# Low parts of 24 weight chunks: a difference on VectorE replaced by a negative on ScalarE and an adding transfer

## The chip, the cores and the metric

The kernel runs on one core of a Trainium2 chip. The metric is the device time of one execution in microseconds (us). The kernel before has a median of 847.87 us over three runs (847.83, 847.87 and 848.68).

## What is computed

One decoder layer for 512 positions of width 1024, in float32: a normalised input goes through one combined projection, three branches use it, their gated sum is projected back and added, and a gated feed-forward part with 2816 hidden columns follows. Cut to what matters here:

```python
h = rmsnorm(x, norm_mix)
qkv_a, a_a, b_a, z_a, glu_in, q_c, gate_logits = split(h @ w_in)
# branch A: gated delta rule on convolved q, k, v, in chunks of 64 (a triangular solve in each)
y_a = (rmsnorm(o_a, gdn_norm) * silu(z_a)) @ w_gdn_out
# branch B: gated linear unit, depthwise convolution of 31 taps, layernorm
y_b = silu(layernorm(conv31(u))) @ w_cc_out
# branch C: attention of 4 heads into mem (256 positions)
y_c = softmax(q_c k_m / sqrt(128)) v_m @ w_xa_out
x = x + (sum of sigmoid(gates) * y) @ w_o
x = x + (silu(conv3(W_g h)) * (W_v h)) @ w_down
return rmsnorm(x, norm_final)
```

## The kernel before

Activations lie in SBUF transposed, 128 features by 512 positions to a tile, and weights come from HBM as 128x128 tiles. A float32 product is made of three matmuls on rounded operands of type float32r: high weight with high activation, high with low, low with high (`proj`, L271 to L273). The high part is the value rounded to float32r, and the low part is what the rounding leaves of it.

So each weight tile is needed as a high and a low part. The array `wall` holds all weights but those of the last projection in the order of their use, as 124 chunks of eight tiles, 128x1024 numbers or 512 KB. `fetch` (L232 to L253) loads a chunk with SP's queue into a `raw` tile (L243), and the helper `split` (L146 to L154) makes the two parts: ACT casts `raw` into `whi` (L150), DVE subtracts `whi` from `raw` into `wlo` (L151). There are four `raw` tiles and four pairs of `whi` and `wlo`, used in turn. `wtile` (L255) calls `fetch` four chunks ahead of the chunk in use, so a pair is written again from the time on at which the chunk four places earlier has been multiplied. Eight tiles of a chunk are 24 matmuls.

The order of PE and of SP's queue is that of the program's text. It is written by generators that are stepped together (`run`), where the projections are the main line and the smaller matmuls of the branches are put between their tiles. The orders of DVE, ACT and POOL come out of the compiler's scheduler, which goes by the dependences and by its own costs.

Chunks with the numbers 22 to 45, counted from 0, hold the second half of the weights of `k`, then those of `q`, `v` and `z` of branch A, and most of the chunks that mix the gates of branch C with its output weights. Their loading and splitting falls in the time from about 97 to 259 us. What else runs there, by line:

- Softmax of the attention scores: DVE's maximum (L523, L524), ACT's exponentials `e` (issued by the helper at L140), DVE's scaling (L530). The transposed probabilities are split into `pTh` on ACT and `pTl` on DVE and multiplied with the values at L549 to L551.
- The gates `gl` of the convolution branch on ACT, `u` on DVE (L598), and 31 taps for each of four tiles on DVE (`cc`, L608). Exponentials and the sigmoid of `gl` need different tables on ACT, so table loads stand between them.
- The decay matrices `dec` of branch A: DVE at L501, exponentials on ACT, a factor on POOL (L712).
- Norms of `k`: POOL's `pow` (L683), DVE's products, and `rows` (L305), which casts a small tile `c` (L308), subtracts (L309) and transposes both on PE (L313).
- The base inverse (L749 to L766): a chain of multiplications and subtractions on the tile `ti` on DVE, which solves the 32x32 triangles. SP stores the result to HBM (L768, L769) and loads it in another layout (L772). `invert` copies it on ACT and POOL (`tm`, `tt`, L794 to L799), makes small products on PE, copies them (`m`, L807) and multiplies again on PE (L813, L814).

Of the kernel before, what the change touches and what calls it, by code (L numbers as in the profile page):

```python
# [11 lines left out]
AF = mybir.ActivationFunctionType  # L12
ALU = mybir.AluOpType
AX = mybir.AxisListType

P = 128
# [4 lines left out]
WAIT = {"mem": 4, "x": 30, "decay": 15, "scores": 1, "level": 6, "scan": 3, "out": 8,  # L21
        "k": 20, "head": 7, "krow": 6, "inverse": 16, "store": 5, "load": 14, "z": 4, "kk": 1, "ln": 30, "mix": 0}
WARM = 10

EARLY = 8

# [33 lines left out]
def hybrid_kernel(ctx: ExitStack, tc: tile.TileContext, xT, memT, xtok, mtok, wall, wdn, nfin, vecs, cms, y):  # L60
# [15 lines left out]
    def nm(p):  # L76
        uid[0] += 1
        return f"{p}{uid[0]}"
# [21 lines left out]
    def G(shape=(P, S)):  # L100
        return psg.tile(list(shape), F32, name=nm("g"), tag="g")
# [4 lines left out]
    A, G_, PE = nc.scalar, nc.gpsimd, nc.tensor  # L106
# [40 lines left out]
    def split(src, hi, lo, scale=None, eng=V):  # L147

        if scale is None:
            A.copy(hi, src)  # L150
            eng.tensor_tensor(lo, src, f(hi), op=ALU.subtract)  # L151
        else:
            A.activation(hi, src, AF.Copy, scale=scale)
            V.scalar_tensor_tensor(lo, src, scale, f(hi), op0=ALU.mult, op1=ALU.subtract)  # L154
# [39 lines left out]
    def vc(n, i=0, w=1):  # L194
        o = VOFF[n][0]
        return vec[:, o + i:o + i + w]
# [16 lines left out]
    ps = G()  # L213
    for _ in range(WARM):
        PE.matmul(ps[:, :P], warm[:, P:2 * P], warm[:, :P], start=True, stop=True)
# [16 lines left out]
    def fetch(upto):  # L232
        if upto > NW and beyond[0]:
            beyond[0](2 * (upto - NW))
        while state[0] < min(upto, NW):
            c = state[0]
            raw = wraw.tile([P, 8 * P], F32, name=nm("raw"), tag="raw")
            n = 4 * P if c < QC else 8 * P
            for o in range(0, 8 * P, n):
                if c < QC:  # L240
                    k = 2 * c + o // n
                    nc.sync.dma_start(x[k], xT[:, k])
                nc.sync.dma_start(raw[:, o:o + n], wall[c][:, o:o + n])  # L243
            hi = wsp.tile([P, 8 * P], F32R, name=nm("whi"), tag="whi")
            lo = wsp.tile([P, 8 * P], F32R, name=nm("wlo"), tag="wlo")
            for o in range(0, 8 * P, n):
                c_ = slice(o, o + n)
                if c < QC:
                    k = 2 * c + o // n
                    split(x[k], xh[k], xl[k], vc("nmix", k))  # L250
                split(raw[:, c_], hi[:, c_], lo[:, c_], eng=nc.vector)
            chunks[c] = (hi, lo)
            state[0] += 1  # L253

    def wtile(i, n=1):  # L255

        fetch(i // 8 + AHEAD)
        hi, lo = chunks[i // 8]
        o = (i % 8) * P
        return hi[:, o:o + n * P], lo[:, o:o + n * P]  # L260
# [74 lines left out]


    fetch(QC)
    nc.sync.dma_start(cm[:, :P], cms[:, :P])
    rx, rm = C((P, NT)), C((P, 2))
# [17 lines left out]
    for i in range(4):  # L357
        nc.sync.dma_start(mraw[i], memT[:, 2 * i:2 * i + 2])
        for k in range(2):
            split(mraw[i][:, k], mh[i][:, k], ml[i][:, k], vc("nmem", 2 * i + k))  # L360
        if i == 1:
            fetch(QC + 1)
# [1029 lines left out]
```

## Time and profile before

| | |
|---|---|
| median of three runs | 847.87 us |
| the profiled execution's own time | 850.48 us |
| its span, first to last instruction | 848.7 us |
| mean granted clock of TensorE | 0.995 |
| DMA traffic | 123.22 MB |

The profile is that of one execution. Busy time of an engine is the time in which it had an instruction under way. In the profile's lists, a group or an instruction names line, engine, operation and its tiles as output<-inputs. A bracket such as [0.41 <-DVE pTl L151] gives the engine's idle time before the instruction and what ended it. The granted clock (PEclk) is 1.00 at full speed.

### The profile page before, as it was taken

Reading aid. Unit: us, or ns where it says so; the run is one execution under the profiler, and the core shown is the slowest. Engines: PE = TensorE matmul, PEld = TensorE weight load, DVE = VectorE, ACT = ScalarE, POOL = GpSimd, SP = SyncE. Lnnn points to the kernel's source line nnn. Section 1 sums busy time; section 2 is a strip of 40 time slices with the busy share of each in tenths; the row PEclk is TensorE's granted clock in tenths of the full one; section 3 lists DMA queues with packets and bytes.
Section 4 is the critical chain, followed back from the end, with each engine's and each line's share of the span. In section 5 each row is a group of like instructions: output and inputs, shape, how many; then the busy total and the mean of one; then the engine's idle time right before and its main releaser. Section 6 shows DMA issues by size and latency. Waiting matters only on the chain.

```text
span 848.7 us, 11144 instructions
## 1 busy us (share of the span) xinstructions
PE 837.2 (99%) x4140; PEld 695.1 (82%) x4140; DVE 606.3 (71%) x954; ACT 388.0 (46%) x669; POOL 87.6 (10%) x101
## 2 busy tenths in 40 slices
PE   9999999999999999999999999999999999999996
PEld 7888788788887888888888888888888888888885
DVE  5885799859988999683266556666666656769863
ACT  7854675534235345452334344333333333657443
POOL 0100002500020001032000031111120110000001
PEclk9999999999999999999999999999999999999998
DMA  9753212242063122322244469696896882275662
GB/s 320 294 183 125 75 51 75 78 121 100 25 166 108 51 75 75 100 74 100 100 149 149 149 163 234 182 209 169 211 222 161 229 206 99 76 222 174 223 186 99
DMA packets 60949, 123.22 MB, mean 145 GB/s; under 512 B 18048, under 2 KB 20352, under 8 KB 60544
## 3 DMA queue, kind: packets, MB, share of 16 engines
q1 hardware_dynamic: 47424, 107.84, 38.0%
q0 software_dynamic: 6336, 11.54, 9.0%
q10 hardware_dynamic: 7136, 3.15, 1.3%
q8 instruction: 32, 0.52, 0.3%
q14 instruction: 21, 0.17, 0.1%
HBM read 118.83 MB, written 26.74 MB: 172 GB/s over the span
## 4 chain that ended last, share of the span: by engine, by line
PE 94%; DVE 4%; issue 1%; ACT 1%; POOL 0%; POOLq 0%; DVEq 0%; ACTq 0%
PE mm L271 19%; PE mm L272 18%; PE mm L273 18%; PE g L272 5%; PE g L273 5%; PE g L271 5%; PE g L1261 2%; PE g L1262 2%; PE g L1263 2%; PE mm L1262 2%; PE mm L1261 2%; PE mm L1263 2%; DVE wlo L151 1%; PE g L570 1%; PE g L572 1%
## 5 line engine op out<-in xcount | busy, mean ns | idle before, releaser
L150 ACT CAST whi<-raw 128x1024 fp32r<-128x1024 f32 (+1 forms) x167 | 171.6, 1028 | 277.1 <-PE mm L272 167.9
L151 DVE TENSOR_TENSOR wlo<-raw,whi 128x1024 fp32r<-128x1024 f32 (+1 forms) x167 | 201.3, 1205 | 77.5 <-ACT whi L150 76.6
L271 PE MATMUL mm<-hh,whi 128*128 128x512 f32 x352 | 142.6, 405 | 0.0
L273 PE MATMUL mm<-hh,wlo 128*128 128x512 f32 x352 | 137.6, 391 | 0.0
L272 PE MATMUL mm<-hl,whi 128*128 128x512 f32 x352 | 137.4, 390 | 0.0
L608 DVE SCALAR_TENSOR_TENSOR cc<-u,vec,cc 128x507 f32<-128x507 f32 (+19 forms) x120 | 86.7, 732 | 1.0
L273 PEld LDWEIGHTS mm<-hh,wlo 128*128 128x128 f32 x352 | 66.1, 188 | 14.3
L271 PEld LDWEIGHTS mm<-hh,whi 128*128 128x128 f32 x352 | 66.3, 188 | 13.1 <-issue 1.5
L272 PEld LDWEIGHTS mm<-hl,whi 128*128 128x128 f32 x352 | 66.4, 189 | 11.5
L271 PE MATMUL g<-fh,whi 128*128 128x512 f32 x176 | 69.1, 392 | 0.0
L271 PE MATMUL mm<-fh,whi 128*128 128x512 f32 x176 | 68.9, 392 | 0.0
L273 PE MATMUL mm<-fh,wlo 128*128 128x512 f32 x176 | 68.6, 390 | 0.0
L273 PE MATMUL g<-fh,wlo 128*128 128x512 f32 x176 | 68.6, 390 | 0.0
L272 PE MATMUL g<-fl,whi 128*128 128x512 f32 x176 | 68.6, 390 | 0.0
L272 PE MATMUL mm<-fl,whi 128*128 128x512 f32 x176 | 68.6, 390 | 0.0
L1096 POOL DMA_DIRECT2D q<-wdn x44 | 36.3, 1000 | 160.1 <-DMA q<-q 97.2
L1163 DVE TENSOR_TENSOR fg<-mm,rfb 128x512 f32<-128x512 f32 x22 | 15.2, 691 | 52.1 <-PE mm L273 52.1
L273 PEld LDWEIGHTS mm<-fh,wlo 128*128 128x128 f32 x176 | 33.1, 188 | 6.9
L273 PEld LDWEIGHTS g<-fh,wlo 128*128 128x128 f32 x176 | 33.0, 188 | 6.9
L272 PEld LDWEIGHTS mm<-fl,whi 128*128 128x128 f32 x176 | 33.1, 188 | 6.7
L271 PEld LDWEIGHTS mm<-fh,whi 128*128 128x128 f32 x176 | 33.0, 188 | 6.8
L271 PEld LDWEIGHTS g<-fh,whi 128*128 128x128 f32 x176 | 33.1, 188 | 6.7
(311 smaller groups left out, 1586.4 us busy)
## 6 DMA issues: line engine op xcount, KB each, us to landing
raw<-wall SPq DMA_DIRECT2D x120, 512.0 KB, 3.4
q<-wdn POOLq DMA_DIRECT2D x44, 256.0 KB, 6.4
raw<-q SPq DMA_DIRECT2D x44, 256.0 KB, 2.9
raw<-wdn SPq DMA_DIRECT2D x33, 256.0 KB, 3.4
q<-wdn SPq DMA_DIRECT2D x22, 256.0 KB, 4.5
q<-q SPq DMA_DIRECT2D x22, 256.0 KB, 4.9
x<-xT SPq DMA_DIRECT2D x16, 256.0 KB, 3.9
raw<-wall SPq DMA_DIRECT2D x8, 256.0 KB, 5.5
```

The source lines that it names most:

```text
L150: A.copy(hi, src)
L151: eng.tensor_tensor(lo, src, f(hi), op=ALU.subtract)
L271: PE.matmul(ps, hi, xh[k], start=(k == 0), stop=False)
L272: PE.matmul(ps, hi, xl[k], start=False, stop=False)
L273: last[0] = PE.matmul(ps, lo, xh[k], start=False, stop=(k == n - 1))
L570: PE.matmul(ps[h], hi, xh[k], start=(k == 0), stop=False)
L608: paced(V.scalar_tensor_tensor(a[:, s:], u[c][:, :S - s], vc("dww", c * 31 + 30 - s), a[:, s:], op0=ALU.mult, op1=ALU.add))
L1096: paced(G_.dma_start(dst[p - 3], b[p - 3], accum_op=ALU.add))
L1163: V.tensor_tensor(g, ps, rfb, op=ALU.mult)
L1261: PE.matmul(ps[m], h[:, o:o + P], hi, start=(p == 0), stop=False)
L1262: PE.matmul(ps[m], h[:, o:o + P], lo, start=False, stop=False)
L1263: last[0] = PE.matmul(ps[m], l[:, o:o + P], hi, start=False, stop=(p == NP - 1))
```

## The change

For the chunks 22 to 45, ACT casts the high part as before, then writes the negative of the raw chunk into the low tile, rounded to float32r. A transfer issued by POOL then reads the chunk a second time from HBM and adds it onto that negative. The sum is the rounding's remainder. DVE's subtraction of these chunks falls away, and `raw` comes free when ACT has read it twice. The other chunks stay as they were. In the changed kernel, the lines after L24 have numbers 2 higher, and those from L246 on 6 higher.

```diff
+ADDED = range(22, 46)
...
             hi = wsp.tile([P, 8 * P], F32R, name=nm("whi"), tag="whi")
             lo = wsp.tile([P, 8 * P], F32R, name=nm("wlo"), tag="wlo")
-            for o in range(0, 8 * P, n):
+            if c in ADDED:
+                A.copy(hi, raw)
+                A.activation(lo, raw, AF.Copy, scale=-1.0)
+                G_.dma_start(lo, wall[c], accum_op=ALU.add)
+            for o in range(0, 0 if c in ADDED else 8 * P, n):
                 c_ = slice(o, o + n)
```

The orders of PE and SP's queue stay. The scheduler lays out ACT, DVE and POOL anew. Three places of this follow. Names carry running numbers, which are one or a few higher in the changed kernel (`whi_1239` is `whi_1240` there).

The first is on ACT, from the exponentials of the decay matrices to the next gate. `e` are exponentials of the scores, with table loads around `gl`. Before:

```order
L140 ACTIVATE dec_884<-dec_884 128x512
L140 ACTIVATE dec_885<-dec_885 128x512
L140 ACTIVATE dec_886<-dec_886 128x512
L140 ACTIVATE e_1129,c_1130<-g_1119,c_1126 128x256 x2
L150 CAST whi_1239<-raw_1237 128x1024
L140 ACTIVATE e_1164,c_1165<-g_1154,c_1161 128x256 x2
L140 ACTIVATE e_1191,c_1192<-g_1181,c_1188 128x256 x2
L150 CAST pTh_1249<-g_1253 128x512
L140 ACTIVATE e_1214,c_1215<-g_1204,c_1211 128x256 x2
L140 ACT_TABLE_LOAD
L140 ACTIVATE gl_1221<-mm_1094,vec 128x512
L150 CAST pTh_1251<-g_1268 128x512
```

In the changed kernel, from the table load ahead of the decay matrices:

```order
L142 ACT_TABLE_LOAD
L142 ACTIVATE e_1130,c_1131<-g_1120,c_1127 128x256 x2
L142 ACTIVATE dec_883<-dec_883 128x512
L142 ACTIVATE dec_884<-dec_884 128x512
L142 ACTIVATE dec_885<-dec_885 128x512
L142 ACTIVATE dec_886<-dec_886 128x512
L249 CAST whi_1240<-raw_1238 128x1024
L250 ACTIVATE wlo_1241<-raw_1238 128x1024
L142 ACTIVATE e_1165,c_1166<-g_1155,c_1162 128x256 x2
L142 ACTIVATE e_1192,c_1193<-g_1182,c_1189 128x256 x2
L142 ACTIVATE e_1215,c_1216<-g_1205,c_1212 128x256 x2
L142 ACT_TABLE_LOAD
```

The pair that stood behind `dec` (`e_1129`, now `e_1130`) is now ahead of it, the scaled copy `wlo_1241` stands behind the cast of its chunk, the last pair of exponentials has moved ahead of the table load, and `pTh_1249` (now `pTh_1251`) follows behind the next `gl` with the other `pTh`.

The second is on DVE, at the end of the base inverse. `ti` and `tmp` are the inverse, `cc` taps of the convolution. Before:

```order
L118 TENSOR_TENSOR tmp_2102<-blk_1855,ti_1849 128x32
L151 TENSOR_TENSOR wlo_2332<-raw_2329,whi_2331 128x1024
L608 SCALAR_TENSOR_TENSOR cc_2277<-u_532,vec,cc_2277 128x504
L118 TENSOR_TENSOR ti_1849<-ti_1849,tmp_2102 128x32
L608 SCALAR_TENSOR_TENSOR cc_2277<-u_532,vec,cc_2277 128x503
L118 TENSOR_TENSOR tmp_2102<-blk_1855,ti_1849 128x16
L608 SCALAR_TENSOR_TENSOR cc_2277<-u_532,vec,cc_2277 128x502
L118 TENSOR_TENSOR ti_1849<-ti_1849,tmp_2102 128x16
L608 SCALAR_TENSOR_TENSOR cc_2277<-u_532,vec,cc_2277 128x501
L118 COPY tit_2165<-ti_1849 128x512
L608 SCALAR_TENSOR_TENSOR cc_2277<-u_532,vec,cc_2277 128x500
L608 SCALAR_TENSOR_TENSOR cc_2277<-u_532,vec,cc_2277 128x499
```

In the changed kernel:

```order
L120 TENSOR_TENSOR tmp_2118<-blk_1866,ti_1860 128x64
L120 TENSOR_TENSOR ti_1860<-ti_1860,tmp_2118 128x64
L120 TENSOR_TENSOR tmp_2118<-blk_1866,ti_1860 128x48
L120 TENSOR_TENSOR ti_1860<-ti_1860,tmp_2118 128x48
L120 TENSOR_TENSOR tmp_2118<-blk_1866,ti_1860 128x32
L120 TENSOR_TENSOR ti_1860<-ti_1860,tmp_2118 128x32
L614 SCALAR_TENSOR_TENSOR cc_1262<-u_487,vec,cc_1262 128x486
L120 TENSOR_TENSOR tmp_2118<-blk_1866,ti_1860 128x16
L614 SCALAR_TENSOR_TENSOR cc_1262<-u_487,vec,cc_1262 128x485
L120 TENSOR_TENSOR ti_1860<-ti_1860,tmp_2118 128x16
L120 COPY tit_2181<-ti_1860 128x512
L614 SCALAR_TENSOR_TENSOR cc_1262<-u_487,vec,cc_1262 128x484
```

The subtraction into `wlo` is gone, and the operations of the inverse stand next to each other where taps stood between them.

The third is POOL's queue, from its last operation ahead of the chunks. `c` with `mhalf` is the `pow` of the norms of `k`. Before:

```order
L298 TENSOR_TENSOR c_193<-c_287,mhalf 128x2
L683 TENSOR_TENSOR c_1225<-c_1225,mhalf 128x4
L742 MEMSET ti_1849 128x512
L747 MEMSET ti_1849 64x16 x2
L683 TENSOR_TENSOR c_1225<-c_1225,mhalf 128x4 x3
L712 TENSOR_TENSOR dec_883<-dec_883,c_1225 128x512
```

In the changed kernel:

```order
L304 TENSOR_TENSOR c_193<-c_287,mhalf 128x2
L251 DMA wlo_1098<-wall 128x1024
L251 DMA wlo_1241<-wall 128x1024
L251 DMA wlo_1313<-wall 128x1024
L251 DMA wlo_1384<-wall 128x1024
L689 TENSOR_TENSOR c_1226<-c_1226,mhalf 128x4
L748 MEMSET ti_1860 128x512
L753 MEMSET ti_1860 64x16 x2
L251 DMA wlo_1469<-wall 128x1024
L689 TENSOR_TENSOR c_1226<-c_1226,mhalf 128x4
L251 DMA wlo_1554<-wall 128x1024
L689 TENSOR_TENSOR c_1226<-c_1226,mhalf 128x4
```

Four transfers stand ahead of the first `pow` and one or two ahead of each further one.

## Rows read from the trace of the kernel before

**Rows 1.** Busy time of each engine: us, share of the span, instructions.

```profile
PE 837.2 (99%) x4140; PEld 695.1 (82%) x4140; DVE 606.3 (71%) x954; ACT 388.0 (46%) x669; POOL 87.6 (10%) x101
```

**Rows 2.** Waits of PE by line: us in total, times, longest.

```profile
PE g L813 <- ACT m L807: 1.2, 2, 0.9
PE sm L313 <- DVE c L309: 0.9, 1, 0.9
PE g L550 <- DVE pTl L151: 0.4, 1, 0.4
```

**Rows 3.** Groups of DVE from 95 to 265 us: busy us, mean ns, idle before.

```profile
L151 DVE TENSOR_TENSOR wlo<-raw,whi 128x1024 fp32r<-128x1024 f32 x24 | 30.2, 1256 | 7.8 <-ACT whi L150 7.6
```

**Rows 4.** DMA queues: packets, MB, share of 16 engines.

```profile
q1 hardware_dynamic: 47424, 107.84, 38.0%
q0 software_dynamic: 6336, 11.54, 9.0%
```

**Rows 5.** DMA issues to landing: SP's weight loads, then POOL's issues of L1096.

```profile
raw<-wall SPq DMA_DIRECT2D x120, 512.0 KB, 3.4
...
L1096 POOL DMA_DIRECT2D q<-wdn x44: 802/812/2692, 499.2 to 694.7; - x44
...
DMA to landing us min/median/max: 4.2/6.4/14.6
```

**Rows 6.** Timeline of ACT, 102 to 115 us: start, us, engine, line, operation.

```profile
102.70 0.69 ACT L140 ACTIVATE gl<-mm,vec 128x512 f32<-128x512 f32 x1
...
105.57 2.19 ACT L140 ACTIVATE dec<-dec 128x512 f32<-128x512 f32 x4 [0.88 <-DVE dec L501]
107.67 0.45 ACT L140 ACTIVATE e<-g,c 128x256 f32<-128x256 f32 x1
...
108.57 1.04 ACT L150 CAST whi<-raw 128x1024 fp32r<-128x1024 f32 x1
109.50 0.47 ACT L140 ACTIVATE e<-g,c 128x256 f32<-128x256 f32 x1
...
112.85 1.28 ACT L140 ACT_TABLE_LOAD   x1
114.15 0.69 ACT L140 ACTIVATE gl<-mm,vec 128x512 f32<-128x512 f32 x1
```

**Rows 7.** Timeline of DVE, 104 to 117 us.

```profile
104.53 0.75 DVE L598 SCALAR_TENSOR_TENSOR u<-u,vec,gl 128x512 f32<-128x512 f32 x1
105.19 1.13 DVE L501 SCALAR_TENSOR_TENSOR dec<-g,c,cm 128x128 f32<-128x128 f32 x4
...
116.16 0.69 DVE L151 TENSOR_TENSOR pTl<-g,pTh 128x512 fp32r<-128x512 f32 x1
```

**Rows 8.** Timeline of PE at 116.90 us.

```profile
116.90 0.50 PE L550 MATMUL g<-pTl,vmh 128*128 128x512 f32 x1 [0.41 <-DVE pTl L151]
```

**Rows 9.** Timeline of PE, 162.5 to 164.1 us.

```profile
162.51 0.39 PE L272 MATMUL mm<-hl,whi 128*128 128x512 f32 x1
162.74 0.39 PE L273 MATMUL mm<-hh,wlo 128*128 128x512 f32 x1
164.04 0.60 PE L313 MATMUL sm<-cm,c 128*8 128x128 f32 x4 [0.92 <-DVE c L309]
```

**Rows 10.** Timeline of DVE at 160.99 us.

```profile
160.99 2.07 DVE L151 TENSOR_TENSOR wlo<-raw,whi 128x1024 fp32r<-128x1024 f32 x1
```

**Rows 11.** Two stretches: length, busy (instructions) by engine, PEclk, DMA share, GB/s.

```profile
162.00:165.00 3.00, 2.08 (x12) 1.39 (x12) 2.96 (x5) 0.32 (x1) 3.00 (x3) 1.00 0.29 76
...
260.00:264.00 4.00, 4.00 (x12) 3.13 (x12) 3.94 (x7) 2.50 (x9) 0.00 (x0) 0.57 0.72 230
```

**Rows 12.** Groups of DVE from 187 to 239 us, during the base inverse.

```profile
L151 DVE TENSOR_TENSOR wlo<-raw,whi 128x1024 fp32r<-128x1024 f32 x9 | 11.0, 1222 | 1.4 <-ACT whi L150 1.4
```

**Rows 13.** Waits of SP's queue, the inverse's store.

```profile
SPq L768 <- DVE ti L118: 25.9, 1, 25.9
```

**Rows 14.** Timeline of ACT at 251 us.

```profile
251.00 0.71 ACT L794 COPY tm<-c 32x256 f32<-32x256 f32 x2 [1.68 <-DMA c<-d_out]
```

## The prediction, made before the changed kernel was run

> **What bounds the kernel now.** I began with the busy time of the engines [rows 1]: PE is busy 837.2 of 848.7 us, so the rest of the span, under 12 us, is all that any change beside PE can win, while every wait that is added in front of a matmul counts in full. DVE has 29% of its time free and ACT 54%, so moving work from one to the other is worth nothing as an average. It is worth what PE waits for DVE or ACT at single places. The second view is therefore PE's waits [rows 2]: 0.9 us at L313 for DVE, 1.2 us in two waits at L813 for ACT's copies `m`, and 0.4 us at L550 for DVE's `pTl`. All lie where the 24 chunks of the change are prepared. The profile puts a matmul down as 0.39 us while its successor starts 0.23 us after it, so each idle time after a full matmul is short by 0.16 us: from the 162.74 matmul to the 164.04 one is 1.30 us, 1.07 over the usual distance, where the wait reads 0.92 [rows 9].
>
> **What the change takes away and adds.** It removes 24 subtractions of 128x1024 from DVE, 30.2 us together, 1256 ns each [rows 3]. ACT gets 24 scaled copies of the same shape. The nearest row is its cast of that shape, after which the next operation begins 0.93 us later [rows 6]: 24 x 0.93 = 22 us. POOL gets 24 transfers of 512 KB. PE's order stays. So PE's time changes only at its waits.
>
> *Do the low parts come in time?* A chunk holds the PE for 24 matmuls x 0.23 = 5.5 us [rows 9], and four chunks' tiles exist, so a pair comes free three chunks, 16.5 us, before its use. Cast, one operation that the order puts between, and the scaled copy take 3 x 0.93 = 2.8 us. That leaves 13.7 us for issue and landing. No row shows an adding transfer. The nearest ones are the 256 KB transfers that POOL issues later: 0.8 us to issue, 6.4 us to land, at worst 14.6 [rows 5]. Below, the plain 512 KB load of the same bytes lands in 3.4 us [rows 5]. POOL's queue takes 9.0% of the engines for 11.54 MB, SP's 38.0% for 107.84 MB [rows 4], 0.78 against 0.35 per MB: 2.2 times the time per byte. At 0.78% of 848.7 us per MB, 0.524 MB hold all 16 engines for 3.5 us, 1.7 more than 256 KB do. I take 6.4 + 1.7 = 8.1 us, with the bounds 3.4 and 14.6. With 0.8 to issue this is 4.8 us early: no cost; the three chunks that PE works on meanwhile are the cover. Without it, at 14.6, a chunk would need (5.5 + 2.8 + 0.8 + 14.6) / 4 = 5.93 us where PE needs 5.5: 0.43 each, up to 10 us for 24.
>
> The Trainium skill speaks against this transfer: SBUF — State Buffer, under "A bandwidth-pool intuition that's wrong (but worth ruling out)", says that a transfer issued by GpSimd waits while DVE holds the SBUF ports that the two share, because its descriptors can't be written, and gives 3100 ns for one of 620 ns. The trace bears it out only in part: POOL's issues are 0.8 us, with one at 2.7 [rows 5]; by the page's ratio the 8.1 us would be an estimated 40 us and the change a large loss.
>
> *The L313 wait.* DVE casts `c`, then works on a chunk's subtraction for 2.07 us from 160.99, and only then makes the second half that L313 waits for [rows 10]. That subtraction goes to ACT, and the two small operations become neighbours. The wait goes: -1.07. The `pow` of POOL ahead of them now has two more transfers before it; 2 x 0.8 us of issue is less than the 2.07 taken out, so I cost it at nothing. The worst is that the 1.07 stays.
>
> *The L813 waits.* They come from far back. The base inverse on DVE is a chain of some 60 small operations, and SP sat 25.9 us on its result [rows 13]. Store, load and ACT's copies follow in order: ACT starts `tm` at 251.00 after 1.68 us idle for that load [rows 14], then has the rest of these copies and two casts ahead of `m`. Between 187 and 239 DVE also made nine subtractions of weights, 11.0 us [rows 12], which leave, and the new order puts the inverse's operations together. All links then come over 10 us sooner, against a wait of 1.2 us. Next late would be nothing that I see. -1.2 - 2 x 0.16 = -1.5.
>
> *The clock behind them.* After these waits and the small matmuls between them, the granted clock in 260 to 264 is 0.57 [rows 11], near the lower of its two levels, 1.2 GHz, and over these 4 us PE loses 0.43 x 4 = 1.7. With the waits gone I expect full speed, 2.4 GHz: -1.7. For it speaks that one gap of 1.07 us alone, in 162 to 165, left the clock at 1.00 [rows 11]; against it, that the small matmuls stay.
>
> *What ACT pays, at 105 to 118.* ACT is busiest here. The new order puts a pair of `e` ahead of the four `dec`, all three later pairs ahead of `gl`, both `pTh` behind it, and a scaled copy into the middle. By hand: the `gl` at 102.70 ends at 103.39 [rows 6]; DVE needs 0.66 for `u`, half of 1.13 for two `dec` [rows 7] and some 0.2 for the small operation that ACT now waits for: 104.8. Then table 1.28, `e` 0.90, `dec` 2.10, cast and scaled copy 1.86, three pairs of `e` 2.70, table 1.28, and `gl` 0.69 [rows 6]: it ends at 115.6, where it ended at 114.84. From there the second L550 followed at 116.90 [rows 8], 2.06 later; now the first `pTl`, 0.69 [rows 7], also stands between. 115.6 + 2.06 + 0.69 = 118.4, so +1.5. If ACT's table load ran ahead of its wait, or DVE, which loses two subtractions here, came sooner, the wait that is there now (0.41 + 0.16) could go: -0.6 is the lower bound. With a further 0.5 us for DVE's work between, +2.0 is the upper.
>
> Sum: 850.48, the profiled execution's own time, + 1.5 - 1.07 - 1.5 - 1.7 = 847.7. That execution is 2.6 above the median of 847.87, and I take the same off: **845.1 us**. A measurement of this kernel tells about 0.2%, 1.7 us, from no change, so faster is below 846.2 and slower above 849.6.
>
> **Rivals.** *A: the clock does not come back.* ACT's price and the 0.57 that is there now make two waits of some 1 us close together at 115 to 118, as the two at L813 are; the granted clock falls there instead, or the small matmuls alone bring it down at 260. One loss of 1.7 stays: 846.8, no change. For it: [rows 11] shows a drop after just such a place.
>
> *B: the gains don't come.* POOL's queue, with the `pow` and the `tt` copies behind transfers that wait for ACT, takes the place of DVE at L313 and L813. Only ACT's price is left: 847.87 + 1.5 = 849.4, no change. Against it: DVE's 30.2 us are gone whatever POOL does, and POOL is busy for 10% [rows 1].
>
> *C: adding is slow.* L273 of the 22nd and later chunks waits for the transfer into `wlo`. It decides from a landing of 13.7 - 0.8 = 12.9 us on; at 14.6 the cost is up to 10 us, 855, and each further us costs 24 / 4 = 6. For it: no row shows an adding transfer, and the 24 hold 24 x 3.5 = 83 us of all engines beside SP's loads. Against it: my landing of 8.1 is well short of the point.
>
> *D: DVE holds POOL's transfers up.* The place and the price are C's, the cause another: what POOL has to write for a transfer waits while DVE works, which it does 71% of the time [rows 1]. At POOL's worst issue and landing, 2.7 and 14.6 [rows 5], a chunk needs (5.5 + 2.8 + 2.7 + 14.6) / 4 = 6.4 us, 0.9 over: up to 22 us, 867. Against it: 0.8 and 6.4 are the medians of 44 with DVE at work. This is the rule of SBUF — State Buffer in the Trainium skill, cited above.
>
> **How the numbers follow.** Forecast 0.46, with its neighbours down to 843.0 (ACT's price at its lower bound, 2.1 less); A 0.22; B 0.11; C 0.13; D 0.08. Faster is the forecast and a little of A where the drop is shorter: 0.48. Same is the rest of A and B: 0.31. Slower is C and D: 0.21. The range runs from 843.0 to 852.4, where C has 17 of the 24 chunks late by 0.43 (7.3 us); beyond it lie D, the other half of C and little at the low end, under 0.2. The forecast's own range is 843.0 to 846.2.
>
> **What would show it.** In the new profile: no wait at L313 and L813, the window 260 to 264 at clock 1.00, two waits of about 1 us at L549 and L550 near 116 to 118, transfers into `wlo` landing near 8 us with no wait at L273. L273 waiting for a DMA proves C or D, and a long issue on POOL beside it D; a clock below 1 after 118 or at 260 proves A; waits on POOL prove B.

## The result, and the profile after

The changed kernel takes 855.53 us (median of 4 runs, 854.97 to 857.55) beside 848.18 us for the kernel before, run with it: a ratio of 1.0089, 95% interval 1.0077 to 1.0101. It is 7.35 us slower, where 2.8 us faster was forecast. The time lies above the range, which ended at 852.4. The profiled execution took 855.82 us, with a span of 854.0.

Busy times and queues of the changed kernel, as in [rows 1, 4]:

```profile
PE 838.5 (98%) x4140; PEld 695.4 (81%) x4140; DVE 585.3 (69%) x930; ACT 410.4 (48%) x693; POOL 103.2 (12%) x125
...
q0 software_dynamic: 9792, 24.12, 17.5%
```

PE does the same work in 5.3 us more span than in the profile of [rows 1]. DVE gave up 21 us and ACT took 22. POOL's queue has doubled its share of the DMA engines. The waits of PE, as in [rows 2]:

```profile
PE mm L277 <- ACT sg L142: 4.5, 1, 4.5
...
PE g L556 <- DVE pTl L153: 0.9, 1, 0.9
PE g L555 <- ACT pTh L152: 0.9, 1, 0.9
```

L313 and L813 are gone, as forecast. Two waits of 0.9 us stand at L555 and L556, forecast too. New and unforeseen is one wait of 4.5 us, in which a matmul of the gates' projection waits for ACT's sigmoid `sg`. POOL's transfers into `wlo`, with the time to issue one (ns, shortest, median and longest) and to its landing, as in [rows 5]:

```profile
L251 POOL DMA_DIRECT2D wlo<-wall x24: 856/865/1079, 99.3 to 268.2; - x24
...
DMA to landing us min/median/max: 5.5/7.8/10.0
```

Median 7.8 us to land, 10.0 at worst: my 8.1 held, and no wait of PE names a transfer. The loss is elsewhere. Stretches of the changed kernel (length, busy us of PE, PEld, DVE, ACT and POOL with instructions, PEclk, DMA share, GB/s; the DMA share is the mean busy share of the 16 DMA engines):

```profile
119.00:122.00 3.00, 3.00 (x11) 2.32 (x10) 3.00 (x5) 0.56 (x1) 0.88 (x1) 0.50 0.63 160
205.00:215.00 10.00, 10.00 (x59) 8.71 (x59) 9.52 (x24) 6.54 (x15) 2.45 (x4) 1.00 0.96 206
215.00:225.00 10.00, 10.00 (x46) 8.26 (x45) 9.24 (x29) 4.50 (x6) 3.30 (x5) 1.00 0.77 157
225.00:235.00 10.00, 10.00 (x54) 8.30 (x52) 9.31 (x14) 4.47 (x5) 1.71 (x2) 1.00 0.92 148
235.00:245.00 10.00, 9.11 (x41) 7.21 (x39) 8.16 (x12) 2.56 (x10) 2.25 (x9) 1.00 0.82 223
248.00:252.00 4.00, 3.41 (x8) 2.74 (x9) 3.52 (x5) 3.95 (x5) 0.86 (x1) 0.57 0.40 94
260.00:264.00 4.00, 4.00 (x42) 3.35 (x37) 3.96 (x7) 1.62 (x3) 0.86 (x1) 1.00 1.05 277
```

Two stretches run at about half clock, 119 to 122 and 248 to 252, while 260 to 264 is at 1.00 (0.57 in [rows 11]). And the DMA engines are busy for 0.77 to 0.96 from 205 to 245, where the kernel before had them at 0.42 and less:

```profile
205.00:215.00 10.00, 10.00 (x57) 8.66 (x57) 9.55 (x23) 1.54 (x2) 2.11 (x4) 1.00 0.28 98
215.00:225.00 10.00, 10.00 (x48) 8.26 (x47) 9.07 (x21) 3.09 (x4) 0.00 (x0) 1.00 0.01 2
225.00:235.00 10.00, 10.00 (x51) 8.31 (x50) 9.41 (x22) 4.09 (x5) 0.00 (x0) 1.00 0.00 0
235.00:245.00 10.00, 10.00 (x46) 8.29 (x45) 9.47 (x16) 1.25 (x2) 1.05 (x2) 1.00 0.42 54
```

In that stretch the result of the base inverse goes out to HBM, the memory outside the core, and comes back; this is called the round trip below. SP's queue in the changed kernel (start, us, instruction), then in the kernel before:

```profile
222.61 0.61 SPq L774 DMA_DIRECT2D d_out<-ti  x1
223.50 3.35 SPq L775 DMA_DIRECT2D d_out<-tit  x1
...
227.68 4.31 SPq L775 DMA_DIRECT2D d_out<-tit  x1
...
234.51 0.39 SPq L778 DMA_DIRECT2D c<-d_out  x1
```

```profile
238.60 0.61 SPq L768 DMA_DIRECT2D d_out<-ti  x1
239.77 0.59 SPq L769 DMA_DIRECT2D d_out<-tit  x1
...
241.25 2.16 SPq L769 DMA_DIRECT2D d_out<-tit  x1
...
245.81 0.39 SPq L772 DMA_DIRECT2D c<-d_out  x1
```

The inverse itself is done 16 us earlier, at 222.6 instead of 238.6. But SP's second and fourth store now hold its queue for 3.35 and 4.31 us instead of 0.59 and 2.16. The stores of `ti` and `tit` land after 6.4 and 7.7 us at the median, where it was 3.7 and 3.8, and the load is issued 11.9 us after the first store instead of 7.2. The load itself lands later too, first before, then changed:

```profile
c<-d_out SPq DMA_DIRECT2D x1, 512.0 KB, 5.1
```

```profile
c<-d_out SPq DMA_DIRECT2D x1, 512.0 KB, 7.8
```

ACT, which has the copies of the loaded tile next in its order, stands still for it:

```profile
242.42 0.71 ACT L800 COPY tm<-c 32x256 f32<-32x256 f32 x2 [8.56 <-DMA c<-d_out]
...
246.39 0.48 ACT L805 COPY tt<-c 32x128 f32<-32x128 f32 x2
...
247.85 0.68 ACT L142 ACTIVATE sg<-mm,vec 128x512 f32<-128x512 f32 x1
```

From the first store to ACT's first copy 19.8 us pass, where before it was 238.6 to 251.0, 12.4 us. ACT waits 8.56 us, copies for 4.5 and casts a chunk, and only at 247.85 comes to the second gate of branch C. That gate reads its input out of one of three `mm` buffers in PSUM, the memory that PE writes its results to. PE needs this buffer for its next product and goes on when the gate has ended:

```profile
243.72 0.39 PE L279 MATMUL mm<-och,wlo 128*128 128x512 f32 x1
248.59 0.79 PE L277 MATMUL mm<-hh,whi 128*128 128x512 f32 x1 [4.47 <-ACT sg L142]
249.18 0.63 PE L278 MATMUL mm<-hl,whi 128*128 128x512 f32 x1
249.60 0.63 PE L279 MATMUL mm<-hh,wlo 128*128 128x512 f32 x1
```

From 243.72 to 248.59 is 4.87 us, 4.64 over the usual distance of 0.23, and the later matmuls begin at half clock, 0.42 apart. In the new order the copies `tm` and `tt` are ahead of that gate, its cast and its scaled copy. Before, four gates of this branch stood ahead of the copies, and the second of them did not wait for the inverse:

```profile
234.89 0.68 ACT L140 ACTIVATE sg<-mm,vec 128x512 f32<-128x512 f32 x1
```

### The profile page after: what moved, and what is told of

The parts are those of the page before. It is cut to its first block, busy times and chain, and to the rows that moved or that the text cites. A ratio compares the mean times of both kernels' runs of the same rounds, so it can differ in the third digit from the quotient of the medians.

```text
span 854.0 us, 11181 instructions
## 1 busy us (share of the span) xinstructions
PE 838.5 (98%) x4140; PEld 695.4 (81%) x4140; DVE 585.3 (69%) x930; ACT 410.4 (48%) x693; POOL 103.2 (12%) x125
## 3 DMA queue, kind: packets, MB, share of 16 engines
q0 software_dynamic: 9792, 24.12, 17.5%
## 4 chain that ended last, share of the span: by engine, by line
PE 68%; DVE 1%; issue 1%; ACT 0%; POOL 0%; POOLq 0%; DVEq 0%
PE mm L277 13%; PE mm L279 13%; PE mm L278 13%; PE g L279 5%; PE g L277 5%; PE g L278 5%; PE g L1269 2%; PE g L1268 2%; PE g L1267 2%; PE mm L1269 2%; PE mm L1268 2%; PE mm L1267 2%; PE g L899 0%; PE g L872 0%; PE sm L1131 0%
## 5 line engine op out<-in xcount | busy, mean ns | idle before, releaser
L152 ACT CAST whi<-raw 128x1024 fp32r<-128x1024 f32 (+1 forms) x143 | 146.7, 1026 | 229.6 <-PE mm L278 132.1
L153 DVE TENSOR_TENSOR wlo<-raw,whi 128x1024 fp32r<-128x1024 f32 (+1 forms) x143 | 171.0, 1196 | 70.8 <-ACT whi L152 69.0
L277 PE MATMUL mm<-hh,whi 128*128 128x512 f32 x352 | 143.9, 409 | 4.5 <-ACT sg L142 4.5
L279 PE MATMUL mm<-hh,wlo 128*128 128x512 f32 x352 | 138.5, 393 | 0.0
L614 DVE SCALAR_TENSOR_TENSOR cc<-u,vec,cc 128x511 f32<-128x511 f32 (+16 forms) x120 | 87.1, 732 | 1.9
L277 PEld LDWEIGHTS mm<-hh,whi 128*128 128x128 f32 x352 | 66.9, 190 | 18.1 <-ACT sg L142 4.9
L279 PEld LDWEIGHTS mm<-hh,wlo 128*128 128x128 f32 x352 | 66.7, 190 | 14.7
L277 PE MATMUL g<-fh,whi 128*128 128x512 f32 x176 | 69.0, 392 | 0.0
L277 PE MATMUL mm<-fh,whi 128*128 128x512 f32 x176 | 68.9, 391 | 0.0
L279 PE MATMUL g<-fh,wlo 128*128 128x512 f32 x176 | 68.6, 390 | 0.0
L279 PE MATMUL mm<-fh,wlo 128*128 128x512 f32 x176 | 68.5, 389 | 0.0
L251 POOL DMA_DIRECT2D wlo<-wall x24 | 21.1, 881 | 164.2 <-ACT wlo L250 154.3
L279 PEld LDWEIGHTS g<-fh,wlo 128*128 128x128 f32 x176 | 33.1, 188 | 7.0
L279 PEld LDWEIGHTS mm<-fh,wlo 128*128 128x128 f32 x176 | 33.0, 187 | 7.0
L278 PEld LDWEIGHTS g<-fl,whi 128*128 128x128 f32 x176 | 33.0, 188 | 6.8
```

The source lines that it names most:

```text
L251: G_.dma_start(lo, wall[c], accum_op=ALU.add)
L277: PE.matmul(ps, hi, xh[k], start=(k == 0), stop=False)
L278: PE.matmul(ps, hi, xl[k], start=False, stop=False)
L279: last[0] = PE.matmul(ps, lo, xh[k], start=False, stop=(k == n - 1))
L614: paced(V.scalar_tensor_tensor(a[:, s:], u[c][:, :S - s], vc("dww", c * 31 + 30 - s), a[:, s:], op0=ALU.mult, op1=ALU.add))
```

## Experiments

**The traffic (e1).** Theory: the adding transfers lengthen the round trip of the inverse, and ACT's order turns that into a wait of PE. Rival: the order alone does it. This run leaves out the five transfers that the changed kernel issues from 208 to 235 us and keeps every order.

```diff
-                G_.dma_start(lo, wall[c], accum_op=ALU.add)
+                if not 36 <= c <= 40:
+                    G_.dma_start(lo, wall[c], accum_op=ALU.add)
```

> Chunks 36 to 40 get no transfer from POOL (their low parts stay the negative of the weights); every instruction of the other engines keeps its place. Theory 'traffic': the changed kernel's transfers in 205 to 245 us fill the DMA engines (share 0.77 to 0.96 there, 0.00 to 0.42 before), so the store and load of the base inverse take 19.8 us from the first store to ACT's first copy instead of 12.4. Without these five transfers they take about 12.4 again, ACT's copies begin by 236, the 4.5 us wait of PE for the gate sg and the half clock behind it (about 1.6) go: 855.5 - 6.2 = about 849.3. Rival 'order': ACT's queue has the copies ahead of the gate, and the gate is late whatever the transfers do: a wait of over 3 us stays, 853 or more.

It took 848.77 us, a ratio of 1.0008 (0.9998 to 1.0017) to the kernel before. ACT's timeline around the first copy and the second gate:

```profile
235.53 0.71 ACT L801 COPY tm<-c 32x256 f32<-32x256 f32 x2 [1.09 <-DMA c<-d_out]
...
240.97 0.69 ACT L142 ACTIVATE sg<-mm,vec 128x512 f32<-128x512 f32 x1
```

With the first store at 223.52 the round trip is 12.0 us, and the load lands after 4.9. The copies begin 6.9 us earlier in ACT's unchanged order, the gate is done at 241.66, and PE's wait is gone. So the order alone does not make PE wait here: the traffic is needed.

**The order (e2).** The same loss from the other side: all transfers stay, the copies are tied behind the second gate.

```diff
+    gates = []
...
+        if ph == 5:
+            gates.append(i)
...
-                A.copy(tm[i][r, :, :, 32 * (b % 2):32 * (b % 2) + 32], tc_[r, 2 * i:2 * i + 2, :, 0])
+                after(A.copy(tm[i][r, :, :, 32 * (b % 2):32 * (b % 2) + 32], tc_[r, 2 * i:2 * i + 2, :, 0]),
+                      gates[1], "behind the second gate")
...
-                    A.copy(tts[t][r, :, r], tc_[r, t, :, 1])
+                    after(A.copy(tts[t][r, :, r], tc_[r, t, :, 1]), gates[1], "behind the second gate")
```

> All transfers stay. On ACT the second gate of branch C, with the cast and the negative beside it, is put ahead of the copies tm and tt. Theory: the wait needs both, the long round trip of the inverse and the place of the gate behind it. The round trip stays near 20 us, the 4.5 us wait and the half clock behind it go: about 849.3. Rival: the delay only moves on, to L819, which waits for ACT's m: a wait there of 2 us or more, 852 to 855.

849.39 us, ratio 1.0010 (1.0000 to 1.0019):

```profile
236.99 0.68 ACT L144 ACTIVATE sg<-mm,vec 128x512 f32<-128x512 f32 x1
...
242.28 0.71 ACT L804 COPY tm<-c 32x256 f32<-32x256 f32 x2 [3.67 <-DMA c<-d_out]
```

The copies start no earlier than in the changed kernel, 242.28 against 242.42, but the gate is done before them, PE does not wait, and nothing came in its place at the later matmuls. Together the two runs show that the 4.5 us need both, the long round trip and a gate queued behind it.

**Adding or placing (e3).** Is it the adding that fills the engines, or would any transfer by POOL?

```diff
-                G_.dma_start(lo, wall[c], accum_op=ALU.add)
+                G_.dma_start(lo, wall[c])
```

> POOL's 24 transfers write the weights into the low tiles instead of adding them (the low part is then the whole weight); all orders stay. If adding is what makes the transfer heavy, POOL's queue falls from 17.5% of the engines toward 9% + 4%, the landing from 7.8 us toward the 3.6 us of SP's loads, the round trip of the inverse gets shorter by several us, and the time falls to 849 to 852. If it is the queue or the size, not the adding: landing near 7.8, 854 to 856.

849.84 us, ratio 1.0021 (1.0012 to 1.0031). POOL's queue, its issues and landings, and ACT's first copy:

```profile
q0 software_dynamic: 9792, 24.12, 13.1%
```

```profile
L251 POOL DMA_DIRECT2D wlo<-wall x24: 527/530/759, 99.9 to 260.9; - x24
...
DMA to landing us min/median/max: 3.6/4.7/6.3
```

```profile
234.59 0.71 ACT L800 COPY tm<-c 32x256 f32<-32x256 f32 x2 [1.74 <-DMA c<-d_out]
```

Placing takes 13.1 - 9.0 = 4.1% of the engines for 24 transfers, where adding takes 17.5 - 9.0 = 8.5%: with spans of 848.2 and 854.0 us that is 1.4 and 3.0 us of all engines for each. The landing goes from 7.8 to 4.7 us, the issue from 0.86 to 0.53, and ACT's wait for the copies from 8.56 to 1.74. So it is the adding. The waits at L555 and L556 were 0.9 us each as in the changed kernel, yet the clock behind them did not fall in the profiled execution:

```profile
119.00:122.00 3.00, 3.00 (x17) 2.49 (x16) 3.00 (x6) 1.70 (x3) 0.54 (x1) 1.00 0.44 141
```

The median is no better than that of e2 all the same. From the start of PE's last matmul to the end of the span its profiled execution took 9.3 us (838.86 to 848.2), that of e2 7.7 (840.10 to 847.8). In it the last wait at the end of POOL's queue (`DRAIN`) took 6.2 us, in e2 and in the changed kernel 4.1; why, and whether the other executions had it, is open.

**ACT's price at 105 to 118 (e4).** Two chunks go back to DVE.

```diff
-ADDED = range(22, 46)
+ADDED = range(24, 46)
```

> Chunks 22 and 23 are split by DVE as before, the rest as changed. ACT's order at 105 to 118 us is then that of the kernel before. Theory: the scaled copy and the new order of the exponentials there cause the two waits at L555 and L556 (2.25 us over the usual distance, 0.57 before) and the granted clock of 0.50 behind them (1.35): 1.7 + 1.35 = 3.0 less, about 852.5, with the 4.5 us wait still there. Rival: the clock falls there anyway, 853.9; or the waits come from the transfers, then nothing changes, 855.5.

853.50 us, ratio 1.0060 (1.0043 to 1.0077). PE's waits and two stretches:

```profile
PE mm L277 <- ACT sg L142: 5.7, 1, 5.7
...
PE g L556 <- DVE pTl L153: 0.4, 1, 0.4
```

```profile
119.00:122.00 3.00, 3.00 (x19) 2.57 (x18) 3.00 (x6) 1.24 (x3) 0.43 (x1) 1.00 0.86 235
246.00:253.00 7.00, 6.05 (x14) 4.78 (x15) 2.64 (x4) 5.22 (x7) 1.73 (x2) 0.52 0.51 115
```

The two waits are down to the 0.4 us of before and the clock in 119 to 122 is full. That is ACT's price, as forecast. The saving in the median is 2.0 us instead of 3.0. In the profile PE comes earlier to the gate while the round trip ends nearly as late: that wait grew from 4.5 to 5.7, and half clock followed for most of 7 us. The profiled execution, at 855.17, is the slowest of the four (853.05 to 855.17), so how much of this the median holds is not shown.

**The half clock in the profile of before (e5, e6).** Part of the forecast hung on one stretch in one execution. The kernel before was profiled twice more.

> The kernel before once more, with a profile. The prediction took the half clock at 260 to 264 us (1.7 us) off the time of every execution, and then the 2.6 us by which the profiled execution was above the median as well. If that drop belongs to this one execution, another profile has none there, and an own time near 848.2; then the change could never win the 1.7, and it was counted twice. If it belongs to the kernel, the new profile has it again.

> The same again, a third profile: the two waits of 0.9 and 1.2 us at L313 and L813 in each profile, the half clock at 260 us in some or in all.

They took 848.22 and 847.63 us. Waits and the stretch of the first, then the stretch of the other:

```profile
PE sm L313 <- DVE c L309: 0.9, 1, 0.9
PE g L813 <- ACT m L807: 0.8, 2, 0.5
```

```profile
260.00:264.00 4.00, 4.00 (x24) 3.10 (x23) 3.88 (x8) 1.80 (x7) 0.00 (x0) 1.00 0.69 224
```

```profile
260.00:264.00 4.00, 4.00 (x32) 3.21 (x31) 3.84 (x8) 1.24 (x5) 0.00 (x0) 1.00 0.78 251
```

Neither has the half clock. The waits are there each time, L313 at 0.9, L813 at 0.8 in the first and 0.6 in the other instead of the 1.2 in [rows 2]. The execution on which the forecast rests was an unusual one of its kernel: of the 48 executions of the kernel before that ran beside the experiments, two took 850.2 us, at a mean granted clock of 0.995 like that one, and the others 847.6 to 849.2, at 0.997 to 0.999.

**Without both losses (e7).** The change with chunks 22 and 23 left to DVE and the copies behind the second gate (the edits of e4 and e2 together).

> Chunks 22 and 23 by DVE and the second gate ahead of the copies, both undone losses together. Theory: neither ACT's price at 105 to 118 (1.7) nor the 4.5 us wait nor a half clock is left; the waits at L313 (1.07) and L813 (1.56) stay away. Against e2 that is 1.7 less, and 1.35 where the drop came: 846.3 to 847.7. Against the kernel before: 2.6 less than its median if its drop at 260 is not in it, 845.6. Rival: the gains of 2.6 do not show in the median, 848.

846.35 us beside 848.15, ratio 0.9980 (0.9971 to 0.9988): faster than both kernels. The profiled execution, at 845.69, is the fastest of the twelve. All that is left of PE's waits in it:

```profile
PE g L221 <- DVE warm L217: 1.5, 1, 1.5
PE g L560 <- DVE pTl L157: 0.4, 1, 0.4
PE g L313 <- POOL c L308: 0.3, 1, 0.3
```

The edits have moved the lines by 10: L313 in this list is L303 of the kernel before, where PE waits 0.3 us for POOL in the profiles of the kernel before too. Its old waits at L313, for DVE's `c`, and at L813 are not among them. The price of ACT at L550 is back at 0.4. The traffic still lengthens the round trip, from 219.60 to 239.00 or 19.4 us, but no wait of PE follows from it.

**And without five of its transfers? (e8)** As e7, but chunks 36 to 40 stay with DVE.

```diff
-ADDED = range(24, 46)
+ADDED = [*range(24, 36), *range(41, 46)]
```

> As e7, but chunks 36 to 40 are split by DVE as before, so no adding transfer runs beside the store and load of the inverse. If the transfers cost nothing once the gate is ahead, this is no faster than e7: 845.6 to 847.7, and round trip near 12 us instead of 19. If the inverse on DVE gets late again by five subtractions (6 us), a wait at L813 comes back: up to 1.5 more.

847.05 us, ratio 0.9988 (0.9980 to 0.9997). The intervals of e7 and e8 overlap, so the two are not told apart. One wait is new in the profiled execution, which at 848.20 is 1.15 above the median:

```profile
PE mm L283 <- DMA wlo<-wall: 1.4, 1, 1.4
```

```profile
242.96 6.14 POOL L808 COPY tt<-c 32x128 f32<-32x128 f32 x8 [6.40 <-DMA c<-d_out]
250.28 0.86 POOL L255 DMA_DIRECT2D wlo<-wall  x1 [1.18 <-ACT wlo L254]
```

With five more chunks on DVE the inverse is later again (SP's first store at 227.83, in e7 at 219.60). The round trip of 12 us did not come: it is 15.1, to ACT's first copy at 242.90. The load is issued 7.1 us after the first store, about as in the kernel before, but it lands after 7.9 us, and the next adding transfer is issued beside it, at 235.70. The copies of its result then fill ACT and POOL, so the adding transfer behind them is issued only at 250.28. It lands 9.1 us later, at 259.36, and the waiting matmul starts at 259.40. It is the only run here in which PE waits for an adding transfer, 1.4 us: late low parts, as in C, mostly by a late issue, for the landing is 1.1 over the median of 8.0. How often this wait comes is not shown. No wait came back at the matmuls of L813.

## Why the prediction was wrong

**Do the low parts come in time?** Right: 8.1 us forecast, 7.8 measured, no wait at L279. C fell with it. But the text says that no row showed an adding transfer, and that is wrong: the transfers of [rows 5] at L1096 are issued with the same adding operation, onto HBM. So the 8.1 was carried over from adding transfers, onto HBM instead of SBUF. And the engine time, 3.5 us forecast for each and 3.0 measured, was used for the transfer's own landing and, under C, beside SP's loads, but not for the inverse's store and load.

**D, and the rule of the skill.** The Trainium skill, SBUF — State Buffer, under "A bandwidth-pool intuition that's wrong (but worth ruling out)", was read as having these transfers wait for whatever DVE does. They did not: 0.86 us to issue, at most 1.08, and 5.5 to 10.0 to land, with DVE busy for 69% of the span and for 82 to 95% of the stretches from 205 to 245. D fell. The passage gives its 3100 ns for a DVE `tensor_copy`, though. Nearly all that DVE did from 200 to 245 us were SCALAR_TENSOR_TENSOR and TENSOR_TENSOR operations, so the passage's own case is not tested here.

**ACT's price.** Right: L555 and L556 stand 1.04 and 1.21 us over the usual distance, 2.25 together, against 0.57 before: +1.7 where +1.5 was forecast. e4 shows the cause. Part of rival A came in addition: a half clock behind these two waits, which cost 3.0 x 0.5 = 1.5 us in 119 to 122.

**The L313 wait.** Right: gone, in all runs with the change.

**The L813 waits.** This is the step that failed. "All links then come over 10 us sooner" carried the store's and the load's times over from a stretch in which the DMA engines stood empty, though the same text had 3.5 us of all engines for each transfer, and five of them were issued from 208 to 235 us. The inverse came 16 us sooner, the copies only 8.6 (242.4 against 251.0): the round trip took 19.8 us, not 12.4. "Next late would be nothing that I see" then overlooked ACT's queue: I had the copies' place relative to the casts, and did not ask which gate stood behind them and when PE would need its buffer. The wait at L813 itself did go. The new one of 4.6 us at L277 and the half clock after it, 3.41 x 0.43 = 1.5 us of busy time, took its place: e1 and e2 bring 6.8 and 6.1 us back.

**The clock.** -1.7 was taken off for a stretch at half clock that the other two profiles of the kernel before do not have. The 1.00 in 260 to 264, forecast for the changed kernel, came, but as those two have it too, the change need not be its cause. Subtracting the 1.7, and then the 2.6 us by which this execution stood above the median, counted it twice. Without that term the forecast would have been 846.8. The sum for the median reads: +1.7 for ACT, -1.07 at L313, about -1.0 at L813 (0.8 and 0.6 in the two profiles, and twice 0.16), +1.5 and +1.5 for the two half clocks, +4.6 at L277: 7.2, where 7.35 was measured. Laid matmul for matmul beside the profile of e5, the changed kernel agrees: PE loses 1.7 at L555 and L556, 1.6 and 1.7 in the two half clocks and 4.6 at L277, gains 1.1 at L313 and 1.1 at L813, and its last matmul comes 7.3 us later.

**The rivals.** B was near in kind, a new wait in place of the old one, but named POOL's queue. It was ACT's and SP's. None of the rivals had the transfers slow down the inverse's store and load, and that decided.

## What to carry to other kernels

A transfer that is hidden for its own user can still lengthen others: here the round trip of the inverse by 7.4 us. Before moving work to the DMA engines, list the round trips through HBM in the stretch where it will run, and price them at the engine time of the new traffic, not at their times of before. Where an engine's order has it wait for such a round trip, read what is queued behind the wait and when its user needs it. And before a term is taken from a clock drop, take a second profile of the kernel before, or leave it out of the sum for the median.

## What the runs showed of the hardware

Adding 512 KB in flight onto SBUF took twice the engine time of placing them by the same queue (3.0 against 1.4 us of all engines), and 7.8 against 4.7 us to land. With five such additions issued from 208 to 235 us the four 128 KB stores of the inverse landed after 6.0 to 8.7 us and its 512 KB load after 7.8; without them (e1) it was 3.4 to 4.2 and 4.9.

The granted clock behind two waits of 0.9 us is not settled by them: it was at half in 119 to 122 in the changed kernel, in e1 and in e2 (0.50, 0.50, 0.51), and full in e3, whose waits at L555 and L556 are the same; each is one execution. The times of one kernel may be spread for this reason: the ten of e2 lie between 847.79 and 848.81 in four cases and between 849.38 and 849.89 in six. The mean granted clock on record for each execution goes with it, 0.998 in the four, 0.996 or 0.997 in the six. Where in the slower ones the clock fell is shown only for the profiled one.
